# A two-layer encoder: the residual's transposes moved into the change of sequence, and squares written to PSUM

## The chip, the cores and the metric

The kernel runs on one core of one Trainium2 chip. The metric is the device time of one execution in microseconds; three runs of the kernel before gave 2633.16, 2638.14 and 2638.25, median 2638.14. A core has TensorE for matrix products (PE; its loads of stationary operands are PEld), VectorE (DVE), ScalarE (ACT), GpSimd (POOL) and SyncE (SP), on whose queue this kernel issues its transfers. Each engine works through its own instructions in order; semaphores couple them. Matmuls write PSUM, and everything else here lives in SBUF or in DRAM.

## The reference, cut to what matters

Two sequences of 512 tokens go through the same two layers, each preceded by 16 learned tokens (528 in all). Layer 1 is a bidirectional gated DeltaNet with 8 heads, layer 2 an attention with 16 heads.

```
h = concat(meta, x)                                  # 528 x 1024
hn = h * rsqrt(mean(h*h, -1) + 1e-6) * ln_g[0]       # the norm of layer 1
proj = hn @ w_in                                     # q, k, v, z and the gates
q, k, v = silu(conv5(proj[qkv])); q, k = l2norm(q), l2norm(k)
o = scan_forward(q, k, v, beta, g) + scan_backward(...)   # chunks, a 128x256 state per head
h = h + (rmsnorm(o) * silu(z)) @ w_out               # the residual
h = h + attention_layer(h)                           # layer 2
```

## The kernel before, in words

All products are done in fp32 by splitting both operands into a high part in fp32r and the rest (names ending in H and L, `wh` and `wl` for weights) and adding three products (`mm3`, lines 72 to 77). The work of layer 1 is cut into 16 units, one per sequence and head. A unit has a front (`gdn_front`: projections of k and q, their convolution, norms, decay matrices and a triangular inverse of 16x16 blocks), `gdn_v` and `gdn_z` (projections of v and z), `gdn_inverse` (the inverse extended from 16 to 128 in steps of small matmuls) and `gdn_scan` (five steps in each direction with the state S). The main loop (line 1160) runs the scan of unit i, and between its steps issues the inverse of unit i+1 and, as filler, the front of unit i+2 and v and z of unit i+1; at i = 6 v and z of unit 7 come first and then front(8).

Front(8) is the change of sequence. It begins with `l1_norm(1)` (line 249), which loads four tiles of 128 tokens, takes their squares, scales the rows, transposes them on PE and writes the result over `hnH` and `hnL`, of which there is one copy each; the projections of unit 7 read the old contents. Then `l1_gates(1)` projects the 32 gate columns, and the projections of unit 8 follow.

The residual of layer 1 needs the unnormalised inputs transposed. `out_transpose_x` (line 750) does it for each sequence in ten groups: half a tile is loaded into `acc`, transposed by four PE instructions into PSUM (`tr`), copied by ACT into another `acc` and stored in DRAM (`hp`). A step of the generator is two groups. The kernel before adds these steps behind the filler of units 10 and 11.

What sets the order: the code is written as generators whose steps are interleaved by hand; a list scheduler then sets each engine's order from the order of the code, priorities (`self.pri`) and its own estimate of times. Tiles of one name rotate through a fixed number of buffers in the order of the code, and a new one waits until its buffer is free: `acc` has four, `raw` two, `wh` and `wl` three, `tr` two in PSUM.

Of the kernel before, what the change touches and what calls it, by code (L numbers as in the profile page):

```python
# [11 lines left out]
AF = mybir.ActivationFunctionType  # L12
# [11 lines left out]
class Trunk:  # L24
# [224 lines left out]
    def l1_norm(self, s):  # L249
        nc = self.nc  # L250
        hh = self.t("hnH", [128, 8, T], F32R)
        hl = self.t("hnL", [128, 8, T], F32R)
        tiles = self.tiles()[s:]
        halves = (slice(0, 512), slice(512, 1024))
        lng = self.t("kq", [128, 1024])
        xs = []
        for j, (i, c0, n) in enumerate(tiles):
            if j == 2:
                nc.sync.dma_start(lng, self.ins["ln_g"][0:1, :].to_broadcast([128, 1024]))
            if s == 0:  # L260
                xs.append(self.load_x(s, i, n, ("B", "D", "B", "D", "kq")[j]))
        for j, (i, c0, n) in enumerate(tiles):
            if s == 0:
                xt = [xs[j][:, c] for c in halves]
            elif j == 0:
                xt = self.load_x(s, i, n, "B")
                xt = [xt[:, c] for c in halves]
            else:
                xt = [self.load_x(s, i, n, "acc", c) for c in halves]
            sc = self.t("sq", [128, 4])  # L270
            ss, rs = sc[:, 0:1], sc[:, 1:2]
            if s == 0:
                junk = self.t("oa", [128, 1024])
                nc.scalar.activation(junk[:n], xs[j][:n], AF.Square, accum_out=ss[:n])
            else:
                s2 = sc[:, 2:4]
                for g, x in enumerate(xt):
                    nc.scalar.activation(hl[:, 4 * g:4 * g + 4, c0:c0 + n], x.rearrange("p (a b) -> p a b", a=4), AF.Square, accum_out=s2[:, g:g + 1])
                nc.vector.tensor_tensor(ss, s2[:, 0:1], s2[:, 1:2], op=ALU.add)
            nc.vector.tensor_scalar(ss[:n], ss[:n], 1.0 / 1024, EPS, op0=ALU.mult, op1=ALU.add)  # L280
            self.rsqrt(rs[:n], ss[:n])
            if s == 0:
                nc.vector.scalar_tensor_tensor(xs[j][:n], xs[j][:n], rs[:n], lng[:n], op0=ALU.mult, op1=ALU.mult)
            else:
                for x, c in zip(xt, halves):
                    nc.vector.scalar_tensor_tensor(x, x, rs, lng[:, c], op0=ALU.mult, op1=ALU.mult)
            for g in range(2):
                ps = self.p(("tr", "lv", "tr", "po")[2 * (j % 2) + g] if s == 0 else "tr", [128, 4, n])
                for k in range(4):
                    nc.tensor.transpose(ps[:, k], xt[g][:n, 128 * k:128 * k + 128], self.ident[:n, :n])  # L290
                nc.scalar.copy(hh[:, 4 * g:4 * g + 4, c0:c0 + n], ps)
                self.sub(nc.vector, hl[:, 4 * g:4 * g + 4, c0:c0 + n], ps, hh[:, 4 * g:4 * g + 4, c0:c0 + n])
            yield
        return hh, hl
# [821 lines left out]
    def run(self, rc, rs):  # L1116
        nc, I = self.nc, self.ins
# [5 lines left out]
        def drain(g):  # L1123
            for _ in g:
                pass
# [4 lines left out]
        def front(i):  # L1130
            s, h = units[i]
            if h == 0:
                cur["hn"] = yield from self.l1_norm(s)
                cur["g"] = self.l1_gates(s, cur["hn"])
                if s == 0:
                    self.setup_vectors()
                yield
            U[i]["hn"] = cur["hn"]
            yield from self.gdn_front(s, h, cur["hn"], cur["g"], U[i])

        def get(f, i):
            return f(i) if i < 16 else iter(())

        v, z, inv = (lambda i: self.gdn_v(U[i])), (lambda i: self.gdn_z(U[i])), (lambda i: self.gdn_inverse(U[i]))
        for f in (front(0), front(1), self.pri(inv(0), 1000), v(0), z(0)):
            drain(f)
# [6 lines left out]
        tx = [self.out_transpose_x(s, hp[s]) for s in range(2)]  # L1153
        def l1_pss():
            pss[0] += [self.p("tr", [128, 264]) for _ in range(2)]
            return
            yield

        pend = []
        for i in range(16):  # L1160
            order = (v, 1), (z, 1), (front, 2)
            if i != 6:
                order = (front, 2), (v, 1), (z, 1)
            fill = chain(*(get(f, i + k) for f, k in order))
            if i in (10, 11):
                fill = chain(fill, tx[i != 10])
            if i == 14:
                fill = chain(fill, (next(op[0]) for _ in range(1)))
            if i == 15:
                fill = chain(l1_pss(), op[0])  # L1170
            iv = self.pri(get(inv, i + 1), 100)
            for n, _ in enumerate(self.pri(self.gdn_scan(U[i], y1[units[i][0]], pend), 100)):
                if n > 0:
                    next(iv, None)
                for _ in range(((1, 1, 1, 1, 1, 1, 1, 1, 1, 1) if i == 15 else (3, 3, 1, 2, 1, 2, 2, 3, 2, 2))[n]):
                    next(fill, None)
            drain(iv)
            if i != 15:
                drain(fill)
# [13 lines left out]
        def head(u):  # L1193
            self.pair_k(u)
            yield
            self.pair_qrope(u)
            yield
            if u["hp"]:
                yield
            self.pair_q(u, 0)  # L1200
            yield
            if u["hp"]:
                self.pair_v(u)
                yield
            self.pair_q(u, 1)
            with ExitStack() as behind:
                for x in [self.last_wl] + ([self.last_mx, self.last_P] if self.last_mx is not None else []):
                    behind.enter_context(self.tc.issue_after(x.ins))
                self.pair_knorm(u, 0)
                self.pair_knorm(u, 1)  # L1210
            yield
            self.pair_z(u, 0)
            yield
            if u["hp"] == 0:
                self.pair_v(u)
                yield
# [15 lines left out]
        fill = chain(self.l2_prep(0, h1[0], rsd[0], ctx[0]), head(units[0]))  # L1232
# [12 lines left out]
        for i, u in enumerate(units):  # L1245
            edge = i % 8 == 7
            if not edge:
                fill = head(units[i + 1])
            else:
                fill = chain(self.l2_prep(1, h1[1], rsd[1], ctx[1]), head(units[8])) if i == 7 else ends[0]  # L1250
# [65 lines left out]
```

## Time and profile before

| | |
|---|---|
| runs, median (lowest to highest) | 2638.14 us (2633.16 to 2638.25) |
| the profiled execution, its span | 2639.61 us, 2637.9 us |
| PE, PEld busy | 2479.0 us (94%), 2225.1 us (84%) |
| DVE, ACT, POOL busy | 1744.4 (66%), 1402.1 (53%), 1159.4 (44%) |
| granted TensorE clock, mean | 0.964 |
| DMA | 321.06 MB, mean 122 GB/s |

Layer 1 fills the first 1320 us or so. A timeline of one engine gives start, duration and operation, with the idle time before it and what ended that in brackets. A table of windows gives the busy time of each engine in a stretch, its granted clock (1.00 is the full 2.4 GHz, 0.50 the lower level of 1.2 GHz) and the share of the DMA engines. Matmuls overlap in the pipeline, so their issue distance, not their duration, is what one costs.

### The profile page before, as it was taken

The numbers are of one execution on the slowest core, as the hardware profiler recorded it, in microseconds if no ns is written. First come the engines' busy times: TensorE is split into PE (matmuls) and PEld (weight loads), VectorE is DVE, ScalarE is ACT, GpSimd is POOL, SyncE is SP. The second block draws the span as 40 slices with busy tenths as digits, with TensorE's granted clock in tenths as the row PEclk, the third lists the DMA queues.
The fourth block names the chain that finished last, engine by engine and source line by source line (L and its number), as shares of the span: only waits on it lengthen the run. The fifth ranks groups of instructions, "written<-read, shape, count | busy, mean of one in ns | idle before, by whom it ended". The sixth has DMA issues, their size and how long they took to land.

```text
span 2637.9 us, 52172 instructions
## 1 busy us (share of the span) xinstructions
PE 2479.0 (94%) x19083; PEld 2225.1 (84%) x19083; DVE 1744.4 (66%) x3915; ACT 1402.1 (53%) x3424; POOL 1159.4 (44%) x1157
## 2 busy tenths in 40 slices
PE   8899999999999999999989899999998999999999
PEld 7878888888888889888989888888887888888787
DVE  5987887776887867875553346767775577666421
ACT  5544556546445554535545356656655556665432
POOL 5544555422333323323445455555445544544243
PEclk9999999989999999989999999999999999999999
DMA  6544545443333355434465423333332333225575
GB/s 200 176 126 136 162 134 152 145 125 94 106 96 104 99 175 145 124 110 144 123 207 171 134 77 75 71 74 80 85 89 77 81 69 73 73 70 150 172 218 148
DMA packets 453216, 321.06 MB, mean 122 GB/s; under 512 B 134812, under 2 KB 364430, under 8 KB 452960
## 3 DMA queue, kind: packets, MB, share of 16 engines
q1 hardware_dynamic: 452960, 317.73, 42.4%
q8 instruction: 150, 2.46, 0.4%
q14 instruction: 106, 0.87, 0.1%
HBM read 216.02 MB, written 92.67 MB: 117 GB/s over the span
## 4 chain that ended last, share of the span: by engine, by line
PE 58%; DVE 20%; DMA 8%; ACT 7%; issue 3%; POOL 3%; SPq 2%; ACTq 0%; POOLq 0%; DVEq 0%
PE pj L75 12%; PE pj L76 12%; PE pj L77 12%; DVE kq L374 2%; DVE acc L374 2%; PE ch L692 2%; DVE Yt L504 1%; PE po L710 1%; PE ch L703 1%; DVE Y L506 1%; DMA acc<-acc 1%; PE tr L1097 1%; PE lv L552 1%; DVE P L1083 1%; PE lv L543 1%
## 5 line engine op out<-in xcount | busy, mean ns | idle before, releaser
L88 POOL TENSOR_TENSOR wl<-wraw,wh 128x512 fp32r<-128x512 f32 (+2 forms) x414 | 535.8, 1296 | 721.5 <-ACT wh L219 628.3
L75 PE MATMUL pj<-hnH,wh 128*128 128x264 f32 (+4 forms) x2080 | 633.4, 306 | 18.4 <-ACT wh L219 5.4
L77 PE MATMUL pj<-hnH,wl 128*128 128x264 f32 (+3 forms) x2080 | 628.9, 304 | 3.2 <-POOL wl L88 2.1
L76 PE MATMUL pj<-hnL,wh 128*128 128x264 f32 (+3 forms) x2080 | 626.7, 302 | 0.6 <-DVE hnL L784 0.6
L75 PEld LDWEIGHTS pj<-hnH,wh 128*128 128x128 f32 (+1 forms) x2080 | 400.1, 193 | 36.8 <-ACT wh L219 5.8
L219 ACT CAST wh<-wraw 128x512 fp32r<-128x512 f32 (+2 forms) x414 | 247.8, 599 | 333.0 <-PE pj L76 193.4
L77 PEld LDWEIGHTS pj<-hnH,wl 128*128 128x128 f32 (+1 forms) x2080 | 399.5, 192 | 18.4 <-POOL wl L88 3.1
L76 PEld LDWEIGHTS pj<-hnL,wh 128*128 128x128 f32 (+1 forms) x2080 | 400.3, 192 | 15.4 <-issue 2.5
L76 PE MATMUL pj<-h2L,wh 128*128 128x512 f32 (+1 forms) x544 | 206.0, 379 | 3.4 <-DVE h2L L88 3.4
L75 PE MATMUL pj<-h2H,wh 128*128 128x512 f32 (+1 forms) x544 | 205.3, 379 | 0.9 <-DVE zs L1059 0.7
L77 PE MATMUL pj<-h2H,wl 128*128 128x512 f32 (+1 forms) x544 | 206.1, 380 | 0.0
L1076 DVE TENSOR_REDUCE mx<-S 128x1 f32<-128x528 f32 x128 | 89.7, 702 | 72.9 <-PE S L1073 72.0
L1080 ACT ACTIVATE P<-S,mx,qs 128x528 f32<-128x528 f32 x128 | 101.4, 792 | 59.4 <-DVE mx L1077 57.5
L1103 ACT CAST hnH<-tr 128x512 fp32r<-128x512 f32 x128 | 75.0, 586 | 98.8 <-PE tr L1097 96.9
L76 PEld LDWEIGHTS pj<-h2L,wh 128*128 128x128 f32 x544 | 102.4, 188 | 23.7 <-DVE h2L L88 4.5
L732 POOL TENSOR_TENSOR oa<-oa,ot 128x256 f32<-128x256 f32 (+1 forms) x80 | 69.6, 870 | 119.7 <-DVE ot L730 111.0
L75 PEld LDWEIGHTS pj<-h2H,wh 128*128 128x128 f32 x544 | 102.4, 189 | 20.3 <-DVE zs L1059 0.9
L77 PEld LDWEIGHTS pj<-h2H,wl 128*128 128x128 f32 x544 | 102.7, 189 | 17.3
L374 DVE SCALAR_TENSOR_TENSOR acc<-raw,vec,acc 128x528 f32<-128x528 f32 x128 | 111.7, 876 | 6.8 <-ACT acc L372 5.7
L374 DVE SCALAR_TENSOR_TENSOR kq<-raw,vec,kq 128x528 f32<-128x528 f32 x128 | 104.8, 819 | 11.7 <-ACT kq L372 10.7
L793 DVE TENSOR_TENSOR raw<-raw,pj 128x512 f32<-128x512 f32 (+1 forms) x54 | 31.3, 579 | 121.0 <-PE pj L77 120.8
L88 DVE TENSOR_TENSOR hnH<-tr,hnH 128x512 fp32r<-128x512 f32 x128 | 88.4, 690 | 18.7 <-ACT hnH L1103 13.4
(483 smaller groups left out, 6834.3 us busy)
## 6 DMA issues: line engine op xcount, KB each, us to landing
wraw<-in_gdn_w_in_dram SPq DMA_DIRECT2D x96, 256.0 KB
wc<-wh SPq DMA_DIRECT2D x96, 256.0 KB
wc<-wl SPq DMA_DIRECT2D x96, 256.0 KB
wh<-wc SPq DMA_DIRECT2D x96, 256.0 KB
wl<-wc SPq DMA_DIRECT2D x96, 256.0 KB
wraw<-in_mla_w_in_dram SPq DMA_DIRECT2D x88, 256.0 KB
wraw<-in_gdn_w_out_dram SPq DMA_DIRECT2D x64, 256.0 KB
wraw<-in_mla_w_out_dram SPq DMA_DIRECT2D x64, 256.0 KB
```

Source lines behind the costliest of these rows:

```text
L75: mm(out, ah, bh, start=first, stop=False)
L76: mm(out, ah, bl, start=False, stop=False)
L77: mm(out, al, bh, start=False, stop=last)
L88: return eng.tensor_tensor(out, a, hi, op=ALU.subtract)
L219: nc.scalar.copy(wh, raw)
L374: nc.vector.scalar_tensor_tensor(acc, raw[:, j:j + T], self.convw(j, u), acc, op0=ALU.mult, op1=ALU.add)
L692: PE.matmul(pc[:n, 0], kq[:, 0, sl], S[d], start=True, stop=True)
L732: G.tensor_tensor(oa[:n, i], oa[:n, i], t, op=ALU.add)
L793: nc.vector.tensor_tensor(r[:, c0:c0 + chunk], r[:, c0:c0 + chunk], ps, op=ALU.add)
L1076: self.last_mx = V.tensor_reduce(mx, Sv, axis=AX.XY, op=ALU.max, negate=True)
L1080: self.last_P = A.activation(P, Sv, AF.Exp, bias=mx, scale=qs[j][:, qt:qt + 1], accum_out=sm)
L1103: A.copy(PTH[:, :, hc], pt)
```

## The change

In `l1_norm`, the squares of the second sequence, of which only the sums are used, are written to a PSUM tile `tr` instead of the part of `hnL` that the norm fills later. In `run`, the twenty groups of `out_transpose_x` leave units 10 and 11 and go into the filler of unit 6: after v and z of unit 7, a new helper advances front(8) by a step and the transposes by one, in turn, until both are used up.

```diff
             else:
                 s2 = sc[:, 2:4]
                 for g, x in enumerate(xt):
-                    nc.scalar.activation(hl[:, 4 * g:4 * g + 4, c0:c0 + n], x.rearrange("p (a b) -> p a b", a=4), AF.Square, accum_out=s2[:, g:g + 1])
+                    nc.scalar.activation(self.p("tr", [128, 512]), x, AF.Square, accum_out=s2[:, g:g + 1])
                 nc.vector.tensor_tensor(ss, s2[:, 0:1], s2[:, 1:2], op=ALU.add)
...
+        def both(a, b):
+            for _ in a:
+                next(b, None)
+                yield
+            yield from b
+
...
             fill = chain(*(get(f, i + k) for f, k in order))
-            if i in (10, 11):
-                fill = chain(fill, tx[i != 10])
+            if i == 6:
+                fill = chain(get(v, 7), get(z, 7), both(front(8), chain(*tx)))
```

The scheduler turns this into other orders on every engine. On PE, where the projections of the second sequence begin, the kernel before has these rows (L692, L713 and L721 are steps of the scan of unit 6, L290 the last transposes of the norm, `32x256` a product for the gates, `pj` of `128x256` the first projection of unit 8):

```order
L660 MATMUL po<-ident,osq 128x128 x2
L713 MATMUL ch_8131<-mV,mW 128x256
L692 MATMUL ch_8588<-S_8130,kq 128x256
L290 MATMUL tr<-ident,acc 128x128 x4
L692 MATMUL ch_8484<-S_8129,kq 128x256
L721 MATMUL po<-mV,mW 16x256
L75 MATMUL pj<-hnH,wh 32x256
L75 MATMUL pj<-hnH,wh 128x256
L76 MATMUL pj<-hnL,wh 128x256
```

The scan of unit 6 has only begun there; it and unit 7's follow between the projections. The same place on PE in the changed kernel (`XF_368` and `S_9623` belong to the scan of unit 7, L757 is a group of the residual's transposes, L311 the transposes of the gates):

```order
L75 MATMUL pj<-hnH,wh 32x256
L76 MATMUL pj<-hnL,wh 32x256
L77 MATMUL pj<-hnH,wl 32x256
L692 MATMUL ch_9884<-S_9623,kq 128x256
L757 MATMUL tr<-ident,acc 128x128 x4
L721 MATMUL po<-mV,mW 16x256
L703 MATMUL ch_9884<-r,XF_368 128x256
L703 MATMUL ch_9965<-r,XF_368 128x256
L311 MATMUL tr<-ident,acc 128x32 x2
L75 MATMUL pj<-hnH,wh 128x256
L76 MATMUL pj<-hnL,wh 128x256
```

Now the whole scan of unit 6, the first steps of unit 7's and eight groups of the residual's transposes stand ahead of the first projection; the other twelve groups stand behind it, between projections. On SP, the queue of transfers in that stretch reads in the changed kernel (`acc<-in_x_sample` loads an input of the norm, `acc<-in_x_prompt` one of the residual, `hp<-acc` stores a copy; the waits are those that the instruction carries, DMAHW for an earlier transfer):

```order
L246 DMA acc<-in_x_prompt_dram 128x512 [waits DMAHW6_49,DVE_49,PE_49]
L760 DMA hp_117<-acc 128x4x128 [waits DMAHW7_49,Activation_49]
L246 DMA acc<-in_x_sample_dram 128x512 [waits DMAHW1_49,DMAHW0_49,PE_49]
L246 DMA acc<-in_x_sample_dram 128x512 [waits DMAHW7_49]
L760 DMA hp_117<-acc 128x4x128 [waits DMAHW2_49,Activation_49]
L246 DMA acc<-in_x_prompt_dram 128x512 [waits DMAHW6_49,DMAHW3_49,PE_49]
L246 DMA acc<-in_x_prompt_dram 128x512 [waits DMAHW4_49,DVE_49,PE_49]
L760 DMA hp_117<-acc 128x4x128 [waits DMAHW5_49,Activation_49]
L663 DMA y_115<-y 128x2x128 [waits DVE_49]
L246 DMA acc<-in_x_sample_dram 128x512 [waits DMAHW3_49,PE_49]
L246 DMA acc<-in_x_sample_dram 128x512 [waits DMAHW4_49,DMAHW0_49,PE_49]
```

In the kernel before, the loads of the norm's tiles stand in this stretch without a store of `hp` between them.

## Rows read from the trace of the kernel before

**Rows 1.** Table of windows: us busy and instructions, clock, DMA share, GB/s.
```profile
564.20:613.40 49.20, 39.32 (x358) 32.11 (x358) 33.90 (x84) 27.82 (x79) 15.04 (x20) 0.72 0.16 41
...
660.00:760.00 100.00, 92.91 (x837) 84.42 (x837) 87.72 (x234) 53.18 (x163) 42.40 (x58) 0.98 0.37 105
920.00:1080.00 160.00, 158.47 (x1475) 144.70 (x1474) 109.70 (x286) 81.25 (x224) 35.45 (x54) 0.98 0.53 156
```

**Rows 2.** Timeline of PE, 555 to 625: start, us, line, operation, tiles.
```profile
564.16 0.28 PE L77 MATMUL pj<-hnH,wl 128*128 128x264 f32 x1
...
593.16 1.06 PE L613 MATMUL tr<-ident,acc 128*128 128x128 f32 x4
...
595.86 1.05 PE L290 MATMUL tr<-ident,B 128*128 128x128 f32 x4
...
602.40 1.12 PE L290 MATMUL tr<-ident,acc 128*128 128x128 f32 x4 [2.32 <-DVE hnL L88]
...
613.43 0.28 PE L76 MATMUL pj<-hnL,wh 128*128 128x256 f32 x1
613.55 0.28 PE L77 MATMUL pj<-hnH,wl 128*128 128x256 f32 x1
```

**Rows 3.** Timeline of ACT, 560 to 625.
```profile
564.36 0.63 ACT L278 ACTIVATE hnL<-B 128x512 fp32r<-128x512 f32 x1 [0.88 <-PE pj L76]
564.89 0.19 ACT L278 ACTIVATION_READ_ACCUMULATOR hnL<-B 128x1 f32 x1
...
594.47 0.36 ACT L617 ACTIVATE vt<-tr,kn 16x128 f32<-16x128 f32 x1 [0.50 <-PE tr L616]
```

**Rows 4.** Timeline of DVE, 560 to 625.
```profile
573.02 1.41 DVE L286 SCALAR_TENSOR_TENSOR acc<-acc,sq,kq 128x512 f32<-128x512 f32 x2 [0.66 <-POOL sq L92]
...
594.76 0.68 DVE L614 TENSOR_TENSOR vt<-tr,kn 128x512 f32<-128x512 f32 x1
...
601.67 0.68 DVE L88 TENSOR_TENSOR hnL<-tr,hnH 128x512 fp32r<-128x512 f32 x1
...
609.09 0.15 DVE L279 TENSOR_TENSOR sq<-sq 128x1 f32<-128x1 f32 x1
609.27 0.15 DVE L280 TENSOR_SCALAR sq<-sq 128x1 f32<-128x1 f32 x1
```

**Rows 5.** Lines 92, 757, 759, 760: count, ns min/median/max, first and last start.
```profile
L92 POOL TENSOR_TENSOR sq<-sq,mhalf x4: 548/550/555, 566.9 to 609.6; 128x1 f32<-128x1 f32 x4
...
L757 PE MATMUL tr<-ident,acc x80: 207/272/417, 926.1 to 1074.3; 128*128 128x128 f32 x64, 16*128 16x16 f32 x16
...
L759 ACT COPY acc<-tr x20: 212/585/587, 926.6 to 1074.7; 128x512 f32<-128x512 f32 x16, 128x64 f32<-128x64 f32 x4
...
L760 SPq DMA_DIRECT2D hp<-acc x20: 360/371/460, 928.1 to 1075.3; - x20
```

**Rows 6.** Chain of work that ended last, 540 to 660: start, us, what.
```profile
564.40 1.56 DMA Td<-Bs
...
594.46 2.97 DMA acc<-in_x_sample_dram
...
614.89 0.44 PE tr L290 x4
616.62 0.43 PE ch L703 x2
```

**Rows 7.** Timeline of SP, 540 to 640: issues of transfers.
```profile
550.49 0.40 SPq L246 DMA_DIRECT2D acc<-in_x_sample_dram x1
...
551.47 2.38 SPq L246 DMA_DIRECT2D acc<-in_x_sample_dram x2
...
594.46 0.33 SPq L246 DMA_DIRECT2D acc<-in_x_sample_dram x1
```

**Rows 8.** Waits of PE, 660 to 700: us in total, times, longest.
```profile
PE pj L75 <- DMA wh<-wc: 1.4, 1, 1.4
PE pj L77 <- DMA wl<-wc: 0.8, 1, 0.8
```

## The prediction

> **What bounds the kernel now.** I read the busy shares first (the table above): TensorE (PE) is busy 94% of the span and no other engine more than 66%, so a change pays where it removes time in which PE is idle or slow. The table of windows finds one such place: between the last projection of the first sequence and the first full projection of the second, a stretch of 49.2 us, PE is busy 39.32 us and its granted clock averages 0.72 [rows 1]. The other two stretches that matter are read in the same view: where the residual's transposes run now, PE is busy 158.47 of 160 us; after the change of sequence, from 660 to 760, it is busy 92.91 of 100 and VectorE (DVE) 87.72, the highest share of DVE anywhere near [rows 1].
>
> The timeline of PE gives the stretch its ends: the last projection of the old sequence starts at 564.16, the transposes of the new sequence's first tile stand at 595.86, those of the second at 602.40, and the first projection with 128 columns of weights is under way at 613.43; I use 613.4 [rows 2]. In between PE finishes the scan of unit 5, the inverse of unit 7 and starts the scan of unit 6. The scans of units 6 and 7 are a backlog: they run after 613 underneath the projections of unit 8.
>
> **The squares.** They now write a PSUM tile "tr" instead of hnL. In the trace the squares of the first tile start at 564.36, released by the last projection that reads hnL [rows 3], but its transposes come at 595.86: 31 us of slack, so releasing the squares from hnL can gain nothing there. The new place has a wait of its own. "tr" has two buffers, handed out in the order of the code, and the two before the squares belong to the last transposes of V of unit 7, which are evacuated by DVE at 594.76 and by ScalarE (ACT) at 594.47 [rows 3, 4]. In the new order those transposes stand in front of the last two steps of the inverse (they start at 593.16 now [rows 2]; I put them near 587), after which come the evacuations, two squares of 0.62 us with 0.19 of read-out each, POOL's power 0.55 and two scalings, 1.41 together [rows 3 to 5]. With the ACT instructions queued between the two squares I arrive at 597.5 for the first tile's transposes, 1.6 later than before. The destination's own speed has no row in this trace; the nearest is the square at 0.62 us into SBUF [rows 3], so the gain lies between nothing and that, and I take nothing.
>
> The Trainium skill ("ScalarE: Activation LUTs", step by step) says that PSUM is the faster destination for ScalarE, with the caveat that this is useful only if TensorE does not need most of PSUM. Here it does need those buffers, and the caveat is what I follow; by the first half alone the sum would fall by some tenths of a microsecond.
>
> **The transposes: what moves.** Twenty groups of four PE transposes, 20 ACT copies of up to 0.585 us, 20 loads and 20 stores leave 926 to 1075 [rows 5]. PE is full there, so that stretch gives back 20 x 0.44 = 8.8 us (four transposes at 0.11 [rows 6]). The order shows that only 8 of the 20 groups now stand before the first projection of the second sequence; the other 12 stand among projections, where PE is full again, and cost what they did. But the larger shift is in the scans: before the first projection of 128 columns the order now holds the whole scan of unit 6 and the beginning of unit 7's, which the kernel before had behind it.
>
> **What is pulled ahead of that projection** (differences of the two orders, each priced at full clock):
> - 31 fp32 matmuls of 256 columns of the scan (L692, L698, L703, L710, L713, L721) at 0.43 [rows 6]: 13.3
> - 45 of the split products (L81 to L83) at 0.12, the distance from 613.43 to 613.55 [rows 2]: 5.4
> - 46 transposes (32 of the residual, 4 of the norm, 10 of the scan's output) at 0.11: 5.1
> - 23 matmuls of the gates at 0.12 and two small transposes: 3.0
>
> Sum 26.8 us of PE work, which need not be done later. It pays if the stretch grows by less.
>
> **How much the stretch grows.** Both the norm and the residual's transposes take tiles "acc", four buffers in the order of the code: two inputs for a tile of the norm, then input, copy, input, copy for the residual. So the second input of the next norm tile has to wait until the first copy of the residual has been stored. This wait is new: before, the second tile's two inputs were issued by SyncE (SP) at 550.49 and just after, and only later ones waited [rows 7]. A round, from the residual's first transposes to those of the next, is then: transposes 0.44, copy 0.585, issue 0.37 [rows 5], store, load 2.97 [rows 6], square and read-out 0.81, two small DVE operations 0.30 [rows 4], power 0.55, scalings 1.41, eight transposes 0.88, evacuation by ACT and DVE (0.585 and 0.68) before the two "tr" buffers come back. Without the store that is 9.6. The landing of a 256 KB store has no row; the small store in the chain took 1.56 and the load of the same size 2.97 [rows 6]; I take 2.3, near the middle, so 11.9. Behind the waiting load, SP holds later loads, stores of y and at last the weights. ACT and DVE also run the scan, in order, and I add 2 us a round for that (0 to 5): 13.9.
>
> The Trainium skill ("DMA: Bandwidth & Descriptors", anatomy of one DMA) says of the GpSimd path that most of a transfer's fixed time is the receipt of the write, heaviest into HBM. No row here shows it for these stores; by it the store would lie at the upper end, 0.7 us more a round.
>
> The first round has a small store (16 rows, copy 0.21): 597.5 + 11.5 + 2 gives 611 for the second tile (602.40 before). Then 624.9 and 638.8. Behind the last tile come its evacuation, the second half of the gates (23 matmuls) and some steps of unit 7's scan, 7 us in all: the first full projection starts at 645.8. The stretch grows by 32.4 us. The scan is not what sets this: it runs between the rounds.
>
> **The sum.** 32.4 - 26.8 = +5.6. For the weights I add 1.3: PE waited 1.4 and 0.8 us for weights after 660 without any of these transfers in the queue [rows 8]; now the loads and stores of 12 groups stand between weights on SP, with stores that wait for ACT. At best this term is zero, at worst I allow 5. For fewer scans beneath the crowded DVE from 660 to 760 I take nothing in the forecast (it is in the first rival). The profiled execution took 2639.6, so 2646.5; the median of the runs is 1.5 lower. Forecast **2645**.
>
> **Rivals.**
> - *The rounds run near their floor* and the relief of DVE shows. With a store of 1.56, the evacuation hidden and no queueing, a round is 9.9 and the first full projection comes near 632: the stretch grows by 18.6, 8.2 less than the work pulled ahead. DVE loses the scans' steps just where it is 88% busy and PE misses 7.1 us [rows 1]. Some of this back: 2631. For it: the old stretch, at clock 0.72 and 80% busy, has room. Against it: every load in the new chain waits for a store. It decides when the first full projection starts before 635. Chance 0.25.
> - *It evens out*: rounds of about 12 us, the first projection at 640, growth equal to the work pulled ahead, 2638. Chance 0.25.
> - *The queue of weights*: the stretch grows as forecast or more (rounds up to 17, first projection at 655, +14.8 by the same sum), and the 24 transfers of the 12 groups hold up the weights in the dense projections that now have no scan beneath them, by 3 to 5 us: 2655. For it: the waits on weights exist already [rows 8]. Against: between 926 and 1075 the same mixture let PE stay 99% busy [rows 1]. Chance 0.15.
> - That the change does not do what it says is settled by the order: 12 of 20 groups fall outside the idle stretch, and its price is in the sum.
>
> The forecast itself has 0.35. About 0.2%, 5.3 us, is what a measurement of this kernel can tell from no change. Faster by more than that: 0.25; within: 0.25; slower: 0.50, from the forecast and the third rival. The range reaches from the first rival with a little more relief, 2629, to the third with the worst weights, 2658; the forecast's own range is 2640 to 2652.
>
> **What would show it.** In the profile after: the first full projection of the second sequence near 646; norm transposes of the last three tiles about 14 us apart instead of 6; squares (L278) or SP's loads released by stores of hp, PE idle and the clock low through 640; the scan of unit 6 ended before the gates; 920 to 1080 without L757, at the same PE share. Wrong if the tiles are 10 us apart or less, if the first projection starts before 635, or if PE's gaps from 660 to 760 vanish. If the first projection is at 646 and the total still falls, my price of the work pulled ahead is wrong.

## The result and the profile after

The changed kernel takes 2658.47 us (median of 4 runs, 2657.48 to 2660.88), the kernel before 2638.19 beside it: ratio 1.0093, interval 1.0070 to 1.0116. It is slower, as forecast, but by 20 us and not 7, and just outside the range. The profiled execution took 2657.5 with a span of 2655.8.

The last projection of the first sequence starts 8.1 us earlier than in [rows 2]. PE's instructions ahead of it come in the same order in both, but less was lost to the granted clock (1.7 us and not 8.5 between the 256th and the 512th projection, in the count explained below); 8.1 is to be added to the times below when they are held against the prediction's. The timeline of PE after (start, us, line, operation, tiles):

```profile
556.02 0.28 PE L77 MATMUL pj<-hnH,wl 128*128 128x264 f32 x1
...
588.90 1.97 PE L290 MATMUL tr<-ident,B 128*128 128x128 f32 x8 [0.21 <-DVE B L286]
604.70 1.14 PE L290 MATMUL tr<-ident,acc 128*128 128x128 f32 x8
...
618.97 0.63 PE L290 MATMUL tr<-ident,acc 128*128 128x128 f32 x4 [0.93 <-DVE acc L286]
...
633.70 1.11 PE L290 MATMUL tr<-ident,acc 128*128 128x128 f32 x4
...
642.51 0.38 PE L75 MATMUL pj<-hnH,wh 128*128 128x256 f32 x1
```

The tiles of the norm (L290) stand 15.8, 14.3 and 14.7 us apart. The windows of the same stretches as in [rows 1] (us busy and instructions of PE, PEld, DVE, ACT, POOL; clock; DMA share; GB/s):

```profile
556.00:642.50 86.50, 73.55 (x531) 55.72 (x529) 55.75 (x132) 50.44 (x138) 25.03 (x34) 0.76 0.29 76
...
660.00:760.00 100.00, 95.09 (x746) 90.31 (x745) 70.91 (x152) 46.79 (x135) 33.30 (x49) 1.00 0.60 176
920.00:1080.00 160.00, 153.56 (x1453) 136.25 (x1452) 110.10 (x321) 76.28 (x221) 43.03 (x69) 0.97 0.35 100
```

The change of sequence grew from 49.2 to 86.5 us. From 660 to 760 DVE fell from 87.72 to 70.91. From 920 to 1080, where the transposes left, PE's share fell with them: 153.56 busy against 158.47 [rows 1]. (Equal times are not equal stages: the first full projection of the second sequence stands 29 us later after the change.) What PE waits for there is mostly DVE, in the scan and the inverse (the longest waits of PE from 920 to 1130: us in total, times, longest):

```profile
PE po L660 <- DVE y L662: 2.9, 2, 2.5
PE po L721 <- DVE y L662: 2.6, 1, 2.6
PE tr L481 <- DVE D L477: 1.6, 1, 1.6
```

**Where it went.** To compare kernels whose parts shift in time, I count the projections of 128 columns from hnH (L75). The 768th is the first full one of the second sequence (642.51 above), the 736th is 32 before it in the first sequence, and layer 1 ends near the 1728th. "Loss" is PE's idle time plus length times (1 - granted clock). Between the 736th and the 1728th the time rises from 836.0 to 859.9 us, the loss from 77.2 to 100.2: nearly all of the increase is loss. Some 10 us of it are added before the 768th and 13 behind it. The measure is rough: time less loss should be PE's own work, the same in every kernel but tx_dup, and comes out between 754 and 767 us for this stretch. A difference of a few us in loss alone says nothing; the times and losses of a row are those of one execution.

| kernel | ratio to before, 95% | 736 to 768: us, loss | 768 to 1728: us, loss |
|---|---|---|---|
| before | 1 | 65.8, 23.6 | 770.2, 53.6 |
| after | 1.0093 (1.0070-1.0116) | 103.2, 33.5 | 756.8, 66.7 |
| after_2 | 1.0115 (1.0075-1.0154) | 100.8, 30.6 | 759.2, 71.7 |
| tx_only | 1.0103 (1.0073-1.0132) | 96.8, 24.9 | 762.4, 67.5 |
| sq_only | 0.9973 (0.9949-0.9997) | 71.6, 20.3 | 748.0, 37.7 |
| sq_only_2 | 0.9953 (0.9933-0.9972) | 66.2, 13.6 | 747.4, 38.6 |
| tx_raw | 1.0085 (1.0055-1.0115) | 83.4, 23.8 | 770.3, 69.8 |
| tx_behind | 1.0060 (1.0033-1.0087) | 74.1, 23.2 | 771.6, 68.8 |
| tx_split | 1.0040 (1.0019-1.0061) | 104.5, 34.2 | 739.1, 49.7 |
| tx_split_2 | 1.0034 (1.0019-1.0049) | 104.6, 34.9 | 739.1, 48.3 |
| tx_late | 1.0072 (1.0048-1.0097) | 104.4, 34.0 | 747.5, 53.9 |
| tx_dup | 1.0154 (1.0104-1.0204) | 104.3, 34.0 | 770.0, 64.2 |
| tx_i7 | 1.0011 (0.9992-1.0031) | 71.6, 21.4 | 762.6, 52.3 |
| tx_split_raw | 0.9934 (0.9912-0.9956) | 79.5, 21.1 | 734.3, 31.7 |
| tx_split_raw_2 | 0.9935 (0.9907-0.9963) | 83.0, 23.6 | 733.8, 31.7 |
| tx_raw8 | 1.0026 (1.0002-1.0050) | 82.8, 24.5 | 758.6, 50.8 |
| tx_split_78 | 0.9950 (0.9927-0.9972) | 83.6, 25.2 | 745.2, 48.2 |

The medians of before beside the four batches of experiments were 2641 to 2645, so ratios are compared. Expectations in us were written against 2638: 0.1% is 2.6 us. Theory A says that the tiles "acc", shared by the norm and the residual, are the cost; theory B, the 12 groups that stand behind the first full projection, between the steps of unit 8's front part; theory S, that the squares cost nothing (in the expectation of tx_only the letter S stands for the opposite).

### The profile page after: what moved, and what is told of

Read it like the earlier page. It is cut to its first block, busy times and chain, and to the rows that moved or that the text cites. A ratio compares the mean times of both kernels' runs of the same rounds, so it can differ in the third digit from the quotient of the medians.

```text
span 2655.8 us, 52195 instructions
## 1 busy us (share of the span) xinstructions
PE 2491.3 (94%) x19083; PEld 2226.0 (84%) x19083; DVE 1737.6 (65%) x3915; ACT 1402.6 (53%) x3424; POOL 1148.8 (43%) x1157
## 4 chain that ended last, share of the span: by engine, by line
PE 38%; DVE 7%; DMA 4%; ACT 4%; POOL 2%; issue 2%; SPq 1%; POOLq 0%; DVEq 0%; ACTq 0%
PE pj L75 9%; PE pj L76 9%; PE pj L77 9%; DMA acc<-acc 1%; PE tr L1097 1%; DVE RL L88 1%; DVE P L1083 1%; DVE acc L951 1%; PE x L76 1%; DMA acc<-h 1%; PE S L76 1%; PE x L77 1%; PE S L1072 1%; PE S L75 1%; PE S L1073 1%
## 5 line engine op out<-in xcount | busy, mean ns | idle before, releaser
L75 PE MATMUL pj<-hnH,wh 128*128 128x264 f32 (+4 forms) x2080 | 631.7, 305 | 19.4 <-DVE P L793 5.4
L77 PE MATMUL pj<-hnH,wl 128*128 128x264 f32 (+4 forms) x2080 | 624.9, 302 | 2.8 <-DMA wl<-wc 2.1
L76 PE MATMUL pj<-hnL,wh 128*128 128x264 f32 (+4 forms) x2080 | 625.9, 301 | 0.0
L75 PEld LDWEIGHTS pj<-hnH,wh 128*128 128x128 f32 (+1 forms) x2080 | 399.3, 192 | 37.2 <-DVE P L793 6.0
L75 PE MATMUL pj<-h2H,wh 128*128 128x512 f32 (+1 forms) x544 | 205.1, 378 | 2.3 <-ACT h2H L860 1.3
L75 PEld LDWEIGHTS pj<-h2H,wh 128*128 128x128 f32 x544 | 102.1, 188 | 21.8 <-ACT h2H L860 1.5
```

What stands on the lines that cost most here:

```text
L75: mm(out, ah, bh, start=first, stop=False)
L76: mm(out, ah, bl, start=False, stop=False)
L77: mm(out, al, bh, start=False, stop=last)
```

## The experiments

**tx_only**: the move, with the squares back in hnL.

```diff
-nc.scalar.activation(self.p("tr", [128, 512]), x, AF.Square, ...)
+nc.scalar.activation(hl[:, 4*g:4*g+4, c0:c0+n], x.rearrange(...), AF.Square, ...)
```

> The move of the transposes alone; the squares write hnL as in the kernel before. Theory S (the squares in PSUM take part of the loss, by waiting for the two tr buffers): 2650 to 2654, norm tiles 2 to 3 us closer together. Rival (the squares are free, the move does it all): 2656 to 2660, the norm tiles 14 to 15 us apart as with both edits.

Measured 1.0103, above both numbers and level with after: beside the move, the place of the squares changes nothing in the total that can be told (736 to 1728: 859.2 and 859.9 us). It does in the change: the norm's tiles start 12.6, 13.1 and 13.4 us apart (15.8, 14.3 and 14.7 in after) and the stretch is 4 to 6 us shorter than in after and after_2, which is the sign of the first expectation, but the time behind it is longer by about as much.

**sq_only, sq_only_2**: the squares alone, transposes as before.

> The squares of the second normalisation go to PSUM, the transposes of the residual stay where they were. Theory S (the squares cost next to nothing: the move is the whole cost): ratio 0.998 to 1.002. Rival (they hold a bank of the transposes' tag for the time of a square and delay the change of sequence): 1.003 to 1.005, with the stretch at the change 4 to 8 us longer than in before.

> The squares alone again, in more rounds: is the gain real? Theory (squares in the transposes' tag put the norm behind the last transposes of unit 7, so that four more half steps of the scan come before the new projections): ratio 0.996 to 0.999, loss between projections 736 and 1728 again 15 us or more below the 77.3 of before. Rival (chance): 0.999 to 1.002.

Alone the squares gain: 0.9973 and 0.9953, both intervals under 1. The first expectation was passed on its good side; the second held in sign and loss (52.1 against 77.2), its ratio a little under the band. The square is indeed quicker into PSUM (line 278 of sq_only, ns min/median/max), 594 ns against the 0.63 us of [rows 3]:

```profile
L278 ACT ACTIVATE tr<-B x2: 587/594/602, 597.0 to 601.0; 128x512 f32<-128x512 f32 x2
```

The Trainium skill ("ScalarE: Activation LUTs", step by step) says that PSUM is the faster destination; this trace agrees by about 30 ns, 0.2 to 0.3 us over eight squares, though the type written changed with the place (fp32r in SBUF, f32 in PSUM), and no run separates the two. The gain is elsewhere. The squares come at 597.0, not at 564.36 [rows 3], and the order then has 53 half steps of the scan (L703) ahead of the first full projection where before had 49, in a stretch that loses less (20.3 and 13.6 against 23.6). Behind it the loss falls from 53.6 to 38; that the earlier steps cause this too was not tested.

**tx_raw**: after, with all tiles of the residual in "raw" and not in "acc".

```diff
-xt = self.load_x(s, i, n, "acc", ...)
+xt = self.load_x(s, i, n, "raw", ...)
-ev = self.t("acc", [128, 4, n])
+ev = self.t("raw", [128, 4, n])
```

> Both edits, but the residual's tiles take the two buffers raw (idle during the norm) instead of acc. Theory A (the norm's inputs wait for the residual's stores because they share acc): tiles of the norm 6 to 9 us apart instead of 14 to 15, the first full projection of the second sequence about 20 us earlier than with both edits, total 2638 to 2646. Rival (the in-order queues of ACT, DVE and SP set the rounds, not the shared buffers): still 12 us and more apart, total 2652 to 2660. What could mask A: raw is also the buffer of the convolutions that follow, and holds back the first ones.

1.0085, outside theory A's total and near the rival's. In the change itself theory A was nearer: the norm's tiles start 12.9, 8.9 and 8.8 us apart, the stretch is 20 us shorter than in after, and its loss went back to 23.8, as before. What was gained was lost behind it (69.8): the late groups now share "raw" with the convolutions of unit 8, as the expectation had feared. Both questions were mixed here; tx_split_raw and tx_raw8 take them apart.

**tx_split, tx_split_2**: only four of the ten steps (8 groups) go into the change, the other 12 groups back into units 10 and 11.

```diff
-fill = chain(get(v, 7), get(z, 7), both(front(8), chain(*tx)))
+seq = chain(*tx)
+fill = chain(get(v, 7), get(z, 7), both(front(8), islice(seq, 4)))
...
+if i in (10, 11): fill = chain(fill, islice(seq, 3) if i == 10 else seq)
```

> Both edits, but only four of the ten steps of the residual (8 of 20 groups, those that stand before the first projection with both edits) stay in the change of sequence; the other six are put back into units 10 and 11. The stretch at the change is as with both edits, about 10 us of lost time more than before. Theory B (the second half of the loss comes from the 12 groups that were mixed into the front of unit 8: they delay it, and with it the inverse and scan of unit 8, so that the scans trail): the later loss goes, total 2646 to 2650. Rival (it comes from the scans of units 6 and 7 having been run ahead, which leaves the projections without cover): 2655 to 2660.

> tx_split again, in the rounds of tx_split_raw, to be set against it. Expected: ratio 1.003 to 1.008 (1.004 on another chip; its neighbour tx_late 1.0072).

1.0040 and 1.0034, as theory B expected: without the 12 groups more than half of the cost is gone, and the loss in the change (34.2, 34.9) is untouched.

**tx_behind**: all 20 groups in unit 6, but behind front(8).

```diff
-fill = chain(get(v, 7), get(z, 7), both(front(8), chain(*tx)))
+fill = chain(get(v, 7), get(z, 7), front(8), chain(*tx))
```

> The squares in PSUM, all 20 groups of the residual in unit 6 but behind the whole front of unit 8, not mixed with it. Theory A and B: the stretch at the change is as in the kernel before (49 us), the scans of units 6 and 7 stay beneath the projections, the front of unit 8 is not delayed: 2636 to 2643. Rival (groups among dense projections cost by themselves, through the queue of weights on SP): 2645 to 2652, with waits of PE for weights of 5 us or more between 640 and 760.

1.0060, worse than either number. The change is as cheap as before (23.2), but 20 groups in 72 us outrun their own tiles, and PE waits for the loads (690 to 860):

```profile
PE tr L757 <- DMA acc<-in_x_sample_dram: 12.0, 7, 2.6
```

With the loads of the learned tokens it is 15.1 us. The changed kernel shows 2.3 us of such waits in all, so this is a fault of the experiment's own and no answer to B.

**after_2**: the changed kernel again, beside the next three.

> The changed kernel again, on the chip and in the rounds of the three below, so that they can be set against it. Expected: ratio to the kernel before 1.006 to 1.011; between the 736th and the 1728th projection of the first layer 855 to 864 us (836.1 in the profile of before). If that stretch lies outside, the two profiles shown so far differed by chance more than the theories do.

1.0115; 736 to 1728 took 860.1 us (859.9 in the first profile). The size is no chance of one execution.

**tx_late**: as tx_split, the 12 groups in units 12 and 13 and not in 10 and 11. **tx_dup**: after, with all 20 groups a second time in units 10 and 11. Rival C of both: units 10 and 11 lack the groups as fill.

```diff
-if i in (10, 11): fill = chain(fill, islice(seq, 3) if i == 10 else seq)
+if i in (12, 13): fill = chain(fill, islice(seq, 3) if i == 12 else seq)
```

```diff
+if i in (10, 11): fill = chain(fill, self.out_transpose_x(i - 10, hp[i - 10]))
```

> As tx_split, 8 groups in the change of sequence, but the other 12 behind units 12 and 13 and not 10 and 11. Theory B (what costs after the change is that 12 groups stand between the steps of unit 8's front part and hold its inverse back): as tx_split, ratio 1.002 to 1.006, idle plus clock loss between projections 768 and 1248 at most 30 us. Rival C (units 10 and 11 miss the groups as work that filled PE's waits): the loss is back with units 10 and 11, idle plus clock loss between 1024 and 1600 at least 32 us (26 to 31 in before and after, 25 in tx_split) and ratio 1.007 to 1.010.

> The changed kernel, and the 20 groups a second time where before had them, in units 10 and 11 (the same bytes are written twice). Theory B: nothing of what was lost comes back, and the doubled work adds its own 8.8 us of PE: ratio 0.002 to 0.004 above that of after_2. Rival C: the groups fill waits, so that the doubled work is free or better: ratio at most that of after_2, and the loss between projections 1024 and 1248 (13.7 us in after) falls to 4 to 7 us.

tx_late is ambiguous: its ratio of 1.0072 is C's number, its losses are B's (28.7 between 768 and 1248, 24.1 between 1024 and 1600); why it is slower than tx_split stays open. tx_dup is clearer: 1.0154, 0.0039 above after_2, though the two intervals overlap, and 15.2 us lost between 1024 and 1248 (15.3 in after_2) where C wanted 4 to 7. In the changed kernel the groups fill no wait there, which speaks against C.

**tx_i7**: all 20 groups beside the front parts of units 9 and 10.

```diff
+if i in (7, 8):
+    fill = chain(*(both(get(f, i + k), tx[i - 7]) if k == 2 else get(f, i + k) for f, k in order))
```

> Both edits, but all 20 groups beside the front parts of units 9 and 10, one step of each in turn, none in the change of sequence. Theory B in its wide form (groups between the steps of any front part hold that unit's inverse back): idle plus clock loss between projections 768 and 1728 at least 60 us (66.5 and 71.7 in the two profiles of the changed kernel, 53.6 in before, 37.7 in sq_only), ratio 1.003 to 1.008. Rival (only unit 8, which comes out of the change without a lead, can't spare the time): at most 50 us, ratio 0.996 to 1.001.

1.0011 and 52.3: between both. Against sq_only it costs 0.4 to 0.6%, so groups between the steps of a front part cost something in other units too, but less than 20 groups cost in the changed kernel.

**tx_split_raw, tx_split_raw_2**: as tx_split, but the 8 groups of the change take tiles from "raw", which nothing else uses there.

> As tx_split (8 groups in the change of sequence, 12 back in units 10 and 11), but the 8 take their tiles from raw and the 12 from acc, so that the norm shares no buffers with them. Theory A (what the 8 groups cost in the change is the wait of the norm's loads for the residual's stores, through acc): idle plus clock loss between projections 736 and 768 at most 27 us (23.7 in before, 20.4 in sq_only, 34.3 in tx_split), ratio to the kernel before 0.997 to 1.001. Rival D (the groups cost by where they stand, whatever buffers they take): the loss stays at 30 us or more, or comes back between 768 and 1728 (49.3 in tx_split, 37.7 in sq_only), ratio 1.003 to 1.006.

> The fastest version again, in more rounds and beside the other two: ratio to the kernel before 0.991 to 0.996, and below 1 with its whole interval.

0.9934 and 0.9935: 1.0% under tx_split with the same groups in the same steps of the code, and the fastest kernel of this study, faster than before and after. Rival D is out; theory A's sign and loss came (21.1 and 23.6, at most 27 expected), and the ratio fell below its band, by more than A had foreseen. The tiles of the norm, in tx_split and then in tx_split_raw:

```profile
602.93 1.32 PE L290 MATMUL tr<-ident,B 128*128 128x128 f32 x8 [0.84 <-DVE B L286]
...
618.38 1.15 PE L290 MATMUL tr<-ident,acc 128*128 128x128 f32 x8
...
632.65 0.63 PE L290 MATMUL tr<-ident,acc 128*128 128x128 f32 x4 [0.93 <-DVE acc L286]
...
647.38 1.11 PE L290 MATMUL tr<-ident,acc 128*128 128x128 f32 x4
```

```profile
593.16 1.97 PE L290 MATMUL tr<-ident,B 128*128 128x128 f32 x8 [0.19 <-DVE B L286]
...
605.25 1.32 PE L290 MATMUL tr<-ident,acc 128*128 128x128 f32 x8 [0.23 <-DVE acc L286]
...
614.04 1.29 PE L290 MATMUL tr<-ident,acc 128*128 128x128 f32 x8
...
622.99 1.29 PE L290 MATMUL tr<-ident,acc 128*128 128x128 f32 x8 [0.47 <-DVE acc L286]
```

15 us apart in the one; 12.1, 8.8 and 9.0 in the other. The tiles are not all that changed: with "raw" the scheduler also put fewer half steps of the scan ahead of the first full projection, 55 and not 59, and so it is between tx_raw8 and after. What is shown is what the choice of tiles costs together with the order that follows from it; the wait and the order were not separated.

With shared tiles SP waits for both users, here in the changed kernel (waits of SP, 580 to 645): the residual's loads for the norm's tile (DVE L286), then the norm's for the residual's stores.

```profile
SPq L663 <- DVE y L662: 41.3, 5, 18.0
SPq L760 <- ACT acc L759: 8.6, 4, 3.9
SPq L246 <- DVE acc L286: 7.0, 2, 5.3
...
SPq L246 <- DMA hp<-acc: 1.9, 2, 1.4
```

```profile
609.06 2.21 SPq L246 DMA_DIRECT2D acc<-in_x_sample_dram  x2
612.59 0.38 SPq L760 DMA_DIRECT2D hp<-acc  x1
613.07 6.89 SPq L246 DMA_DIRECT2D acc<-in_x_prompt_dram  x2
623.95 0.38 SPq L760 DMA_DIRECT2D hp<-acc  x1
625.45 0.38 SPq L663 DMA_DIRECT2D y<-y  x1
625.91 0.91 SPq L246 DMA_DIRECT2D acc<-in_x_sample_dram  x2
```

The first line is longer than these: stores of y that wait for the scan's result. They stand in the same queue in tx_split (23.2 us from 596 to 655) and in tx_split_raw (31.1 from 580 to 640), so they do not make the difference between the two; what the change would cost without them in this queue was not tested. The second fence is SP's timeline: two loads of the residual (x_prompt) take 6.89 us to issue, and the norm's next loads (x_sample) come only behind the store at 623.95.

**tx_raw8** (the 8 in "raw", the 12 in "acc" between front(8)'s steps, as in after) and **tx_split_78** (the 12 behind the front parts in units 7 and 8).

```diff
 # tx_raw8, against tx_split_raw
-fill = chain(get(v, 7), get(z, 7), both(front(8), islice(seq, 4)))
+fill = chain(get(v, 7), get(z, 7), both(front(8), flip()))   # flip: 4 steps in raw, then the rest in acc
-if i in (10, 11): ...
```

```diff
 # tx_split_78, against tx_split_raw
-if i in (10, 11): fill = chain(fill, islice(seq, 3) if i == 10 else seq)
+if i in (7, 8): fill = chain(fill, islice(seq, 3) if i == 7 else seq)
```

> The changed kernel's order of groups (8 in the change, 12 between the steps of unit 8's front part), but the 8 take tiles from raw, as in tx_split_raw; the 12 take acc. Against tx_split_raw only the place of the 12 differs. Theory B (the 12 hold unit 8's front part and inverse back, the scan stands at its 64th half step until the 1025th projection and is late from there): loss between projections 768 and 1728 at least 50 us (31.7 in tx_split_raw, 66.5 and 71.7 in after), ratio to the kernel before 0.998 to 1.004. Rival A2 (the shared tiles acc are the whole cost, and the 12 cost only through them): at most 40 us, ratio 0.992 to 0.996.

> As tx_split_raw, but the 12 groups stand behind the front parts in units 7 and 8 (among the same projections as in the changed kernel or the ones just behind them), where no front part waits for them. Theory B: ratio 0.992 to 0.996, loss between 768 and 1728 at most 42 us. Rival Q (groups among these projections cost by their loads, stores and copies, held back or not): at least 50 us, ratio 0.998 to 1.003.

tx_raw8 1.0026 and 50.8, tx_split_78 0.9950. The same 12 groups cost 0.9% between the steps of unit 8's front part, and 0.15% (within the intervals) behind it. All three kernels have 55 half steps of the scan ahead of the first full projection, so this comparison is of the place of the groups alone. Theory B holds in the times; its bound on tx_split_78's loss (42) was missed, 48.2, of which 19.2 is idle time (32.0 in tx_raw8, 16.3 in tx_split_raw) and the rest clock. By the loss tx_split_78 would be level with tx_raw8; by the time behind the 768th projection it is 13.4 us shorter (745.2 against 758.6), and its median is 0.8% lower. How it works is read from DVE and the scan. Windows of all engines from 640 to 700, in before, after, tx_raw8 and tx_split_78:

```profile
640.00:700.00 60.00, 57.00 (x415) 52.67 (x414) 52.00 (x126) 34.77 (x110) 30.94 (x41) 0.97 0.37 110
```

```profile
640.00:700.00 60.00, 59.80 (x458) 56.90 (x457) 29.79 (x58) 25.01 (x60) 5.39 (x13) 0.97 0.69 206
```

```profile
640.00:700.00 60.00, 59.44 (x469) 56.82 (x470) 33.84 (x70) 33.08 (x88) 9.23 (x20) 1.00 0.66 201
```

```profile
640.00:700.00 60.00, 60.00 (x459) 56.66 (x457) 52.08 (x118) 35.19 (x113) 26.97 (x37) 1.00 0.41 123
```

And the scan's L703 alone on PE (busy us and count), from 700 to 760 and to 820, in the same four:

```profile
700.00:760.00 60.00, 3.77 (x12) 1.00 0.37 103
760.00:820.00 60.00, 4.20 (x14) 0.94 0.31 88
```

```profile
700.00:760.00 60.00, 0.59 (x2) 1.00 0.50 147
760.00:820.00 60.00, 1.74 (x6) 0.89 0.41 111
```

```profile
700.00:760.00 60.00, 1.19 (x4) 1.00 0.44 129
760.00:820.00 60.00, 1.79 (x6) 1.00 0.47 132
```

```profile
700.00:760.00 60.00, 1.84 (x6) 0.91 0.48 135
760.00:820.00 60.00, 3.67 (x12) 0.88 0.38 108
```

In the kernels with groups inside the front part (the second and third of each four), PE is full from 640 to 700 while DVE gets only 58 or 70 instructions instead of 118 or 126: what feeds DVE, unit 8's convolutions and inverse, stands behind the groups. The inverse's L590 runs 16 times between 700 and 760 in before and tx_split_78 and not once in after and tx_raw8 (busy us and count, in the same four):

```profile
700.00:760.00 60.00, 0.93 (x16) 1.00 0.37 103
700.00:760.00 60.00, 0.00 (x0) 1.00 0.50 147
700.00:760.00 60.00, 0.00 (x0) 1.00 0.44 129
700.00:760.00 60.00, 0.96 (x16) 0.91 0.48 135
```

The four do not begin the second sequence at the same time (613.3, 642.5, 632.0 and 627.6), but counted from there the picture stays: in the 60 us behind the 768th projection DVE gets 96, 58, 71 and 105 instructions, and unit 8's inverse (its first L590) begins 119, 157, 162 and 120 us behind it.

The scan, which had run ahead in the change, has no inverse to go on with: 8 and 10 instructions of L703 in 120 us instead of 26 and 18. From there it trails, and PE meets waits on DVE as those shown above from 920 on.

The groups' own PE work does not explain such a delay: the 12 cost 5.3 us of PE at 0.44 each. In tx_raw8 they start about 5 us apart (648.1 to 704.9), and unit 8's first transposes (L412) stand behind 102 projections of the second sequence, where tx_split_78 has 36. Groups and front part also share the two PSUM tiles "tr", handed out in the order of the code, so that the front part's transposes have to take their turn behind groups that run at the pace of their loads and stores. Whether it is this sharing or the place alone that delays the front part, no run separates.

## Why the prediction was wrong, point by point

- **What bounds, the order, the first tile.** Right. 588.90 plus 8.1 is 597.0 (forecast 597.5).
- **The rounds.** Right in kind, short in size: 44.8 us for the three (41.3 forecast), the first full projection at 650.6 on the old clock of events (645.8). The stretch grew by 37.3 (32.4). PE work without loss between the 736th and the 768th projection rose by 27.4 (69.6 against 42.2; 26.8 forecast), although one price was misread: the 0.43 us of [rows 6] belong to two matmuls of the scan. After the change 57 more of them stand there than before, about 0.215 us apart when they follow each other, 12.3 us and not 13.3. Net +10, not +5.6. I had the norm's load waiting for the residual's store; the SP rows show the other half as well, the residual's loads waiting for the norm's tile, with stores queued behind them.
- **"The other 12 stand among projections, where PE is full again, and cost what they did."** This step failed. The 12 cost 0.9%, some 24 us (tx_raw8 against tx_split_raw), because unit 8's front part comes late through them and not by their own work. The order showed where they stood; I priced them only on PE and did not ask which chain they delay.
- **"For fewer scans ... I take nothing in the forecast."** Failed with it, and with it the idea that work pulled ahead is saved at its price. Behind the 768th projection the time fell by 13.4 us (770.2 to 756.8), not by the 26.8 that were pulled ahead. In tx_split the loss behind the change is 49 against 31.7 in tx_split_raw, with 59 half steps of the scan ahead and not 55. In the first rival I had counted the relief of DVE from 660 to 760 as a gain; it did come (70.91 against 87.72), and was no gain: DVE was starved there and late afterwards. That rival's sum does not come out either: 2638 less 8.2 is 2630 before any relief, so its 2631 holds none.
- **Weights +1.3.** Not what happened. In the rest of layer 1 PE waits 2.5 us for wl and wh after, 2.4 before. The third rival's number lay nearest, its mechanism did not show.
- **8.8 us back from 926 to 1075.** The PE work did leave, but PE's share there fell with it: 153.56 of 160.
- **The squares, nothing.** True of the total beside the move, false alone (-0.3 to -0.5%). Slack of the first tile was the wrong thing to go by: with their later start more of the scan goes first.
- **The sum by medians.** From tx_split_raw (0.9935), the 12 groups in front(8) lead to 1.0026 and "acc" for the 8, with the order that comes with it, to 1.0093 and 1.0115: 0.9% and 0.7 to 0.9%, 24 and 18 to 24 us. Of the shared tiles' cost about 10 us shows in the change (loss of after less tx_raw8: 9.0 and 6.1; tx_split less tx_split_raw: 13.1 and 11.3), the rest behind it.

Open: why the squares alone lower the loss far behind the change, and why the share of "acc" costs as much behind the change as in it; the four more half steps of the scan ahead of it are a candidate that was not tested. Whether a store lands in 2.3 us, as taken from rows, or later, as by the Trainium skill ("DMA: Bandwidth & Descriptors", anatomy of one DMA), where the receipt of the write is most of a transfer's fixed time, no run here separates from the other parts of a round.

## What to carry over

Before work is put between the steps of a producer, ask who waits for that producer: among instructions that keep PE full, the 12 groups cost little behind the front part that feeds DVE and much between its steps. When two streams share a ring of tiles, each can wait for the other's loads and stores; giving the moved stream tiles that are idle at that point turned 0.4% slower into 0.7% faster. Work pulled ahead into a gap did not come back at its price here, because the stretch behind it then lacked work that feeds DVE.

## What the hardware showed beside it

Identical code does not meet the same clock in each execution: from the 256th to the 512th projection, which none of these edits touches, the stretch took 189.9 us in after (1.7 us lost to the clock, 6.2 idle) and 200.2 in tx_i7 (10.2 lost, 9.4 idle). That is the size of many effects here; one profile of each kernel would not have settled them. A square of 128 x 512 by ScalarE took 594 ns into PSUM as f32 (after) and 628 into SBUF as fp32r (before).
